# An expert block on one core: all six low halves of an expert's weights on VectorE, both halves of its output scaled by ScalarE

## The chip, the cores and the metric

The kernel runs on one core of one Trainium2 chip. The metric is the device time of one execution in microseconds (us), smaller is better. The engines are named as in the profile: PE is TensorE, PEld its weight loads, DVE is VectorE, ACT is ScalarE, POOL is GpSimd, SP is the engine that issues most DMAs.

## What is computed

One layer of an encoder block on 512 tokens of width 1024, all in float32: a norm, one wide projection, a gated delta rule (branch A), a sparse attention with an indexer (branch B), their gated sum through an output projection, and then a mixture of experts, which the change concerns:

```python
def hier_moe(h, w_rg, b_rg, w_re, b_re, w1, w3, w2):
    ...                                   # top-1 of 4 groups, then top-2 of its 4 experts
    act = jax.nn.silu(jnp.einsum("nd,edf->nef", xt, w1)) * jnp.einsum("nd,edf->nef", xt, w3)
    act = act * comb[:, :, None].astype(act.dtype)
    y = jnp.einsum("nef,efd->nd", act, w2)
    return y.reshape(bsz, s, d)
```

There are 16 experts, each with w1 and w3 of 1024 x 256 and w2 of 256 x 1024. A final norm follows.

## The kernel before

**Split products.** Every float32 matrix product is made of three products of a shorter format. `split` (line 151) makes a high half with an ACT copy (line 154) and a low half, source minus high half, with a subtraction on a chosen engine (line 155); `mm3` multiplies high x high, high x low and low x high. In the trace the weights' halves are `whi` and `wlo`, 128 x 1024 each. So every piece of the weights costs one ACT and one DVE or POOL instruction before PE can use it.

**The weights as a stream.** `plan` (from line 216) lists all pieces of weights in the order of use, each with its sources and with the engine that makes its low half. `feed_raw` issues the loads on SP, `feed` calls `halves` (line 293), which takes a pair of buffers and calls `split`. An expert has six pieces: four with 256 rows of w1 and w3 side by side, and two halves of w2. In `plan` the w2 pieces of an expert come behind the four pieces of the next one (lines 250 to 253). The engine of the low half is `(DVE, POOL, DVE)[i % 3]`, so pieces 1 and 4 of each expert go to POOL and the other four to DVE: 32 of the 96 pieces on POOL. The halves lie in a ring of six pairs of buffers, the raw pieces in a much longer one.

**One expert.** The loop from line 1686 goes over the 16 experts. Up to 128 tokens of an expert are gathered from DRAM by an indirect DMA on POOL (`gather`, line 1372), two experts ahead. `turn` transposes them on PE (line 1528) and `halves_x` writes their halves (`xhl`, ACT at line 1534, DVE at line 1535). `up` makes 24 products of 128 x 512. `glu` is the Silu on ACT (line 1547) and a product on DVE (line 1548); both write `a`. Then `finish` runs the expert before: `down` (line 1568) makes two outputs of 128 x 512, six products each, and scales them by the tokens' weights into `yb`: the left half on DVE (line 1573), the right half on ACT (line 1571). `scatter` (line 1576) adds `yb` into DRAM, again an indirect DMA on POOL. Last, `turn_a` transposes `a` on PE (line 1554) and splits it into `ah` (ACT) and `al_` (DVE). PE thus runs, for each expert: 24 products with eight transposes of the next expert's tokens among them, 12 products of the expert before, two transposes of `a`.

**The last two experts** are not scattered: `finish` keeps their scaled halves in SBUF (lines 157 and 158), and `combine` multiplies them with 0/1 matrices, which come from `sel` tiles (DVE, line 1368) transposed on PE (line 1706). In the sixth expert `more_tiles` (from line 1590) counts on DVE, in about 18 small instructions, whether an expert has more than 128 tokens; the code for such an overflow (`further`) is in loops at the end, whose instructions do not show up in the profiled execution.

**The order of instructions** on each engine is made by the tile framework when the program is built, so a change of an instruction's engine also moves others. Each engine then runs its own list in order.

Of the kernel before, what the change touches and what calls it, by code (L numbers as in the profile page):

```python
# [10 lines left out]
AF = mybir.ActivationFunctionType  # L11
OP = mybir.AluOpType
# [87 lines left out]
def body(tc, x, positions, norm1_g, w_in, w_proj_a, w_proj_b, w_out, norm2_g,  # L100
# [3 lines left out]
    PE, ACT, DVE, POOL, SP = nc.tensor, nc.scalar, nc.vector, nc.gpsimd, nc.sync  # L104
# [71 lines left out]
    def acc_tile():  # L176
        return pacc([128, 512], name="acc", tag="acc", bufs=4)
# [38 lines left out]
    plan, raws, ready, state = [], [], [], {"at": 0, "limit": None}  # L216
# [27 lines left out]
    def expert_pieces(w1, w3, w2):  # L244
        return [[w[sub * 256:(sub + 1) * 256, :] for w in (w1, w3)] for sub in range(4)] + [
            [w2[:, cb * 512:(cb + 1) * 512]] for cb in range(2)]

    W1, W3, W2 = w_exp_gate[0], w_exp_up[0], w_exp_down[0]

    order = [(e + d, i) for e in range(-1, 16) for d, i in ((1, 0), (1, 1), (1, 2), (1, 3), (0, 4), (0, 5)) if 0 <= e + d < 16]  # L250
    for e, i in order:
        o = ORDER[e]
        plan.append(("ex", expert_pieces(W1[o], W3[o], W2[o])[i], (DVE, POOL, DVE)[i % 3]))
    state["limit"], state["rawlimit"] = NIN + 4, NIN + 1
    LATE0 = NIN + 8 + 3 + NRAW
    late = [(stream, 3)] * 2
# [542 lines left out]
    def t8(name, pool=M):  # L799
        return pool([128, T, 8], name=name)  # L800

    beta, gg = t8("beta"), t8("gg")
    al, ex, u1, sp = (t8(n, AT_) for n in ("al", "ex", "u1", "sp"))
# [415 lines left out]
    def e1(shape, name, dt=F32):  # L1219
        return E1([128] + shape, dt, name=name)  # L1220
# [15 lines left out]
    for fb in range(4):  # L1236
        acc = acc_tile()
# [21 lines left out]
    nm, ex, sums, wn = e1([T, 2], "nm"), e1([T, 24], "exl"), e1([T, 3], "sums"), e1([T, 16], "wn")  # L1259
# [164 lines left out]
    for t in range(T):  # L1424
        acc = acc_tile()
# [134 lines left out]
    def product(al2, w):  # L1560
        ah, al_ = al2
        hi, lo, n = w
        acc = acc_tile()
        for k in range(2):
            mm3(acc, ah[:, k], al_[:, k], hi[:, k], lo[:, k], k == 0, k == 1)
        return acc

    def down(al2, y, cb, w, wtc):
        acc = product(al2, w)
        if cb:  # L1570
            ACT.activation(y[:, cb * 512:(cb + 1) * 512], acc, AF.Copy, scale=wtc)
        else:
            DVE.tensor_scalar(y[:, cb * 512:(cb + 1) * 512], acc, wtc, None, op0=OP.mult)

    def scatter(y, idc):
        return ins_of(POOL.indirect_dma_start(out=accd, out_offset=bass.IndirectOffsetOnAxis(ap=idc, axis=0), in_=y, in_offset=None,  # L1576
# [41 lines left out]
    def further(kv):  # L1618
        ek = SP.value_load(eki[0:1, bass.ds(kv, 1)], min_val=0, max_val=15)
        sl = ohk[:, bass.ds(kv, 1), :].to_broadcast([128, T, 16])  # L1620
        ofs = E2([128, 1], name="ofs", tag="ofs", bufs=1)
        DVE.tensor_copy(ofs, offk[:, bass.ds(kv, 1), :].rearrange("p a b -> p (a b)"))
        t16 = E2([128, T, 16], name="t16", tag="t16", bufs=1)
        pk_ = E2([128, T, 1], name="pk_", tag="pk_", bufs=1)
        rwf = E2([128, T, 2], name="rwf", tag="rwf", bufs=1)
        rwk = E2([128, T, 4], F32R, name="rwk", tag="rwk", bufs=1)
        for src, dst in ((posm, pk_), (f32(WT[:, :, :, 0]), rwf[:, :, 0:1]), (f32(WT[:, :, :, 1]), rwf[:, :, 1:2])):
            DVE.tensor_tensor(t16, src, sl, op=OP.mult)
            DVE.tensor_reduce(dst, t16, axis=AX.X, op=OP.add)
        DVE.tensor_copy(rwk[:, :, 0:2], C("tok")[:, :, None].to_broadcast([128, T, 2]))  # L1630
        DVE.tensor_copy(rwk[:, :, 2:4], rwf)
        DVE.tensor_scalar(pk_, pk_, ofs, None, op0=OP.subtract)
        idk = E2([128, 1], I32, name="idk", tag="idk", bufs=1)
        wtk = E2([128, 1], name="wtk", tag="wtk", bufs=1)
        look_up(slots_of(lambda t: pk_[:, t]), rwk, idk, wtk)
        gather(idk, xeb[0])
        for hf in range(2):
            turn(xeb[0], 0, hf)
        w = lambda W: W[bass.ds(ek, 1)].rearrange("e k c -> (e k) c")
        pieces = expert_pieces(w(W1), w(W3), w(W2))  # L1640
        acc = acc_tile()
        for sub in range(4):
            up(acc, 0, sub, halves(*load(pieces[sub]), DVE))
        al2 = turn_a(glu(acc))
        for cb in range(2):
            down(al2, yb[:, 0], cb, halves(*load(pieces[4 + cb]), DVE), wtk)
        scatter(yb[:, 0], idk)
# [11 lines left out]
    def finish(e):  # L1659
        if e < 16 - NP:  # L1660
            y = yb[:, e % 2]
            for cb in range(2):
                down(act[e], y, cb, chunk(e, 4 + cb), wts[:, ORDER[e]:ORDER[e] + 1])
            sent.append(scatter(y, ids[:, ORDER[e]:ORDER[e] + 1]))
            for i in range(max(0, e - 3), e):
                tc.declare_no_dep(sent[e], sent[i], reason="tokens of another group")
            return
        yhl[e] = yh, yl = spare_tile(F32R), spare_tile(F32R)
        for cb in range(2):
            split(yh[:, half[cb]], yl[:, half[cb]], product(act[e], chunk(e, 4 + cb)), scale=wts[:, ORDER[e]:ORDER[e] + 1])  # L1670
# [15 lines left out]
    for e in range(16):  # L1686
        acc = acc_tile()
# [107 lines left out]
```

## Time and profile before

| | |
|---|---|
| three runs | 748.82, 749.26 and 755.03 us; median 749.26 |
| the profiled execution | 749.99 us, span in the trace 747.9 us |
| mean granted TensorE clock | 0.966 |
| experts' stage (first product to last) | about 541 to 727 us |
| busy over the span | PE 669.9, DVE 553.6, ACT 408.2, POOL 352.5 us |

How to read it. The page cuts the span into 40 slices and groups instructions by line, engine and tile. A group's row ends with its busy time, the mean of one instruction in ns, then the time for which its engine stood idle just before it and what it was waiting for. A timeline row has the start, the duration, the engine, the line and the tile, and in brackets the idle time ahead of it and the instruction that ended it. A row of the stretches (windows) has the length and then for each engine its busy time and in brackets its number of instructions; then the granted clock, the DMA engines' busy share and GB/s. The average over the span says little here, because the stages have different limits; the stage of the experts has to be read by itself.

### The profile page before, as it was taken

The numbers are of one execution on the slowest core, as the hardware profiler recorded it, in microseconds if no ns is written. First come the engines' busy times: TensorE is split into PE (matmuls) and PEld (weight loads), VectorE is DVE, ScalarE is ACT, GpSimd is POOL, SyncE is SP. The second block draws the span as 40 slices with busy tenths as digits, with TensorE's granted clock in tenths as the row PEclk, the third lists the DMA queues.
The fourth block names the chain that finished last, engine by engine and source line by source line (L and its number), as shares of the span: only waits on it lengthen the run. The fifth ranks groups of instructions, "written<-read, shape, count | busy, mean of one in ns | idle before, by whom it ended". The sixth has DMA issues, their size and how long they took to land.

```text
span 747.9 us, 10556 instructions
## 1 busy us (share of the span) xinstructions
PE 669.9 (90%) x3460; PEld 544.0 (73%) x3460; DVE 553.6 (74%) x1112; ACT 408.2 (55%) x722; POOL 352.5 (47%) x300
## 2 busy tenths in 40 slices
PE   3999887889989999999799998999989997899792
PEld 3888666557757777778579998888967776687661
DVE  4562789999985556536954776656799998999785
ACT  5443365585979653443233423343558875888544
POOL 3217526456222212554451114731459985999343
PEclk9999988999999999999899999999999998999997
DMA  7333111112011223225144008697799999995233
GB/s 254 110 107 107 57 57 57 56 58 85 29 57 57 57 61 89 60 74 157 56 132 151 1 2 312 236 345 261 249 308 311 317 301 317 299 292 154 55 122 114
DMA packets 84025, 110.76 MB, mean 148 GB/s; under 512 B 17435, under 2 KB 57883, under 8 KB 83840
## 3 DMA queue, kind: packets, MB, share of 16 engines
q1 hardware_dynamic: 79360, 101.70, 42.2%
q0 software_dynamic: 4320, 7.77, 4.4%
q8 instruction: 28, 0.46, 0.3%
q10 hardware_dynamic: 288, 0.59, 0.2%
q14 instruction: 29, 0.24, 0.1%
HBM read 101.22 MB, written 16.78 MB: 158 GB/s over the span
## 4 chain that ended last, share of the span: by engine, by line
PE 45%; DVE 30%; DMA 11%; issue 7%; ACT 3%; POOL 2%; SPq 1%; DVEq 0%; ACTq 0%; POOLq 0%
PE acc L130 32%; PE pm L130 5%; DVE wlo L155 5%; DVE xh L447 4%; DVE ltmp L938 3%; DVE sn L595 3%; DVE m L594 3%; DVE sn L585 2%; ACT whi L154 2%; DMA g<-in_w_exp_up_dram 2%; DMA g<-in_w_exp_down_dram 2%; DVE X L939 1%; DMA spare<-in_w_exp_up_dram 1%; DMA x<-in_x_dram 1%; PE po L130 1%
## 5 line engine op out<-in xcount | busy, mean ns | idle before, releaser
L155 POOL TENSOR_TENSOR wlo<-raw,whi 128x1024 fp32r<-128x1024 f32 (+1 forms) x56 | 144.7, 2593 | 147.1 <-ACT whi L154 142.4
L154 ACT ACTIVATE whi<-raw 128x1024 fp32r<-128x1024 f32 (+1 forms) x123 | 127.4, 1049 | 111.3 <-PE acc L130 88.5
L155 DVE TENSOR_TENSOR wlo<-raw,whi 128x1024 fp32r<-128x1024 f32 (+1 forms) x67 | 115.6, 1738 | 38.9 <-ACT whi L154 37.4
L130 PE MATMUL acc<-hTh,wlo 128*128 128x512 f32 x224 | 90.9, 407 | 6.2 <-DVE wlo L155 5.8
L130 PE MATMUL acc<-hTh,whi 128*128 128x512 f32 x224 | 91.9, 410 | 5.1 <-ACT xh L445 4.2
L130 PE MATMUL acc<-whi,xhl 128*128 128x512 f32 x256 | 94.0, 420 | 0.3 <-DVE xhl L1535 0.3
L130 PE MATMUL acc<-hTl,whi 128*128 128x512 f32 x224 | 90.3, 403 | 0.0
L130 PEld LDWEIGHTS acc<-whi,xhl 128*128 128x128 f32 x256 | 49.8, 195 | 10.6 <-DVE xhl L1535 0.8
L130 PEld LDWEIGHTS acc<-hTh,whi 128*128 128x128 f32 x224 | 43.9, 196 | 18.1 <-ACT xh L445 5.0
L130 PEld LDWEIGHTS acc<-hTh,wlo 128*128 128x128 f32 x224 | 43.6, 195 | 17.1 <-DVE wlo L155 7.0
L130 PE MATMUL acc<-wlo,xhl 128*128 128x512 f32 x128 | 51.5, 402 | 0.0
L130 PEld LDWEIGHTS acc<-hTl,whi 128*128 128x128 f32 x224 | 43.5, 194 | 10.3 <-issue 1.7
L130 PE MATMUL acc<-whi,hTh 128*128 128x456 f32 (+1 forms) x120 | 46.2, 388 | 0.0
L130 PE MATMUL acc<-wlo,hTh 128*128 128x456 f32 (+1 forms) x120 | 44.9, 374 | 0.0
L130 PE MATMUL acc<-whi,hTl 128*128 128x456 f32 (+1 forms) x120 | 44.7, 373 | 0.0
L1576 POOL DMA_INDIRECT accd<-yb,ids x14 | 32.0, 2283 | 10.0 <-ACT ah L154 4.3
L1372 POOL DMA_INDIRECT xe<-h2d,ids x15 | 24.4, 1629 | 13.2 <-PE pm L1528 9.2
L447 DVE SCALAR_TENSOR_TENSOR xh<-xrb,sm,xh 128x511 f32<-128x511 f32 (+2 forms) x36 | 30.2, 895 | 0.0
L594 DVE MAX8 m<-sn 128x8 f32<-128x256 f32 (+2 forms) x48 | 26.7, 557 | 2.1 <-POOL sn L587 1.4
L130 PE MATMUL acc<-wlo,ah 128*128 128x512 f32 x64 | 26.5, 415 | 1.8 <-DVE wlo L155 1.8
L130 PEld LDWEIGHTS acc<-wlo,xhl 128*128 128x128 f32 x128 | 25.2, 197 | 3.9
L938 DVE TENSOR_TENSOR ltmp<-X,LN 128x31 f32<-128x31 f32 (+15 forms) x31 | 21.0, 676 | 8.7 <-DMA LN<-lane_n 7.8
(472 smaller groups left out, 1708.4 us busy)
## 6 DMA issues: line engine op xcount, KB each, us to landing
raw<-in_w_in_dram SPq DMA_DIRECT2D x24, 512.0 KB
raw<-in_w_exp_gate_dram SPq DMA_DIRECT2D x42, 256.0 KB
raw<-in_w_exp_up_dram SPq DMA_DIRECT2D x42, 256.0 KB
raw<-in_w_exp_down_dram SPq DMA_DIRECT2D x21, 512.0 KB
raw<-in_w_in_dram SPq DMA_DIRECT2D x16, 256.0 KB
raw<-in_w_out_dram SPq DMA_DIRECT2D x8, 512.0 KB
raw<-in_w_in_dram SPq DMA_DIRECT2D x8, 456.0 KB
x<-in_x_dram SPq DMA_DIRECT2D x4, 512.0 KB
```

The source lines that it names most:

```text
L130: return ins_of(PE.matmul(o, l, r, start=start, stop=stop, skip_group_check=True))
L154: h = ins_of(ACT.activation(hi, src, AF.Copy))
L155: return h, ins_of((lo_eng or DVE).tensor_tensor(lo, src, f32(hi), op=OP.subtract))
L447: DVE.scalar_tensor_tensor(xh[:, j:], xr[:, :512 - j], cw[:, blk, 3 - j:4 - j], xh[:, j:], op0=OP.mult, op1=OP.add)
L585: DVE.scalar_tensor_tensor(s, r[:, :N], iwn[:, h:h + 1], s, op0=OP.mult, op1=OP.add)
L594: DVE.max(m8, sn[t])
L595: DVE.match_replace(out=sn[t], in_to_replace=m8, in_values=sn[t], imm_value=-2 * BIG)
L938: DVE.tensor_tensor(tv, skew(flat[0], 0, n, d, 1), skew(flat[1], d, n, d, 32), op=OP.mult)
L939: DVE.tensor_reduce(skew(flat[0], d, n, 1, 1), tv, axis=AX.X, op=OP.add)
L1372: return ins_of(POOL.indirect_dma_start(out=xe, out_offset=None, in_=h2d[0:128 * tiles], in_offset=bass.IndirectOffsetOnAxis(ap=idc, axis= ...
L1576: return ins_of(POOL.indirect_dma_start(out=accd, out_offset=bass.IndirectOffsetOnAxis(ap=idc, axis=0), in_=y, in_offset=None, bounds_chec ...
```

## The change

Both edits are in the stage of the experts. The low halves of all six pieces of each expert are made by DVE. Both halves of `yb` are scaled by ACT.

```diff
@@ -250,7 +250,7 @@
     for e, i in order:
         o = ORDER[e]
-        plan.append(("ex", expert_pieces(W1[o], W3[o], W2[o])[i], (DVE, POOL, DVE)[i % 3]))
+        plan.append(("ex", expert_pieces(W1[o], W3[o], W2[o])[i], DVE))
@@ -1567,10 +1567,7 @@
     def down(al2, y, cb, w, wtc):
         acc = product(al2, w)
-        if cb:
-            ACT.activation(y[:, cb * 512:(cb + 1) * 512], acc, AF.Copy, scale=wtc)
-        else:
-            DVE.tensor_scalar(y[:, cb * 512:(cb + 1) * 512], acc, wtc, None, op0=OP.mult)
+        ACT.activation(y[:, cb * 512:(cb + 1) * 512], acc, AF.Copy, scale=wtc)
```

The lines below the second edit have numbers smaller by three in the changed kernel. The lists of the engines change as follows.

DVE, from the third expert's tokens to the `a` of the fourth (a row is line, operation, output<-inputs, shape; `wlo` is a low half of weights and the tile behind the arrow the place of the raw piece; `xhl` tokens, `al_` the low half of `a`). Before:

```order
L1548 TENSOR_TENSOR a<-a,acc 128x256
L1573 TENSOR_SCALAR yb<-acc,wts 128x512
L155 TENSOR_TENSOR wlo<-xr_4268,whi 128x1024
L155 TENSOR_TENSOR al__5469<-pm,ah 128x256
L155 TENSOR_TENSOR wlo<-spare_4882,whi 128x1024
L155 TENSOR_TENSOR wlo<-xr_4270,whi 128x1024
L1535 TENSOR_TENSOR xhl_5115<-pm,xhl_5115 128x512
L155 TENSOR_TENSOR wlo<-xr_4272,whi 128x1024
L1535 TENSOR_TENSOR xhl_5115<-pm,xhl_5115 128x512
L1548 TENSOR_TENSOR a<-a,acc 128x256
```

And changed:

```order
L1548 TENSOR_TENSOR a<-a,acc 128x256
L155 TENSOR_TENSOR wlo<-raw,whi 128x1024 x2
L155 TENSOR_TENSOR al__5469<-pm,ah 128x256
L155 TENSOR_TENSOR wlo<-xr_4268,whi 128x1024
L155 TENSOR_TENSOR wlo<-spare_4882,whi 128x1024 x2
L1535 TENSOR_TENSOR xhl_5115<-pm,xhl_5115 128x512
L155 TENSOR_TENSOR wlo<-xr_4270,whi 128x1024
L1535 TENSOR_TENSOR xhl_5115<-pm,xhl_5115 128x512
L1548 TENSOR_TENSOR a<-a,acc 128x256
```

From one `a` to the next the list holds six low halves instead of four and no `yb`; two low halves now stand ahead of `al_` instead of one and a `yb`, and `a` still follows the second `xhl` directly.

ACT, in the same place, from the Silu of an expert to the next one's tokens (`whi` is a high half of weights). Before:

```order
L1547 ACTIVATE a<-acc 128x256
L154 ACTIVATE whi<-xr_4268 128x1024
L154 ACTIVATE whi<-spare_4882 128x1024
L1571 ACTIVATE yb<-acc,wts 128x512
L154 ACTIVATE ah<-pm 128x256
```

And changed:

```order
L1547 ACTIVATE a<-acc 128x256
L154 ACTIVATE whi<-xr_4268 128x1024
L1570 ACTIVATE yb<-acc,wts 128x512
L154 ACTIVATE whi<-spare_4882 128x1024
L1570 ACTIVATE yb<-acc,wts 128x512
L154 ACTIVATE ah<-pm 128x256
```

The left half of `yb` comes in between the two high halves, so that one high half, the right `yb` and `ah` stand behind it.

POOL, from the gather of the fourth expert's tokens on (`accd<-yb` is the scatter). Before:

```order
L1372 DMA xe_4279<-h2d,ids 128x1024
L155 TENSOR_TENSOR wlo<-raw,whi 128x1024
L1372 DMA xe_4278<-h2d,ids 128x1024
L155 TENSOR_TENSOR wlo<-raw,whi 128x1024 x2
L1576 DMA accd<-yb,ids 512x1024
L155 TENSOR_TENSOR wlo<-raw,whi 128x1024
L1372 DMA xe_4279<-h2d,ids 128x1024
L155 TENSOR_TENSOR wlo<-spare_4882,whi 128x1024
L1576 DMA accd<-yb,ids 512x1024
```

And changed:

```order
L1372 DMA xe_4279<-h2d,ids 128x1024
L1372 DMA xe_4278<-h2d,ids 128x1024
L1573 DMA accd<-yb,ids 512x1024
L1372 DMA xe_4279<-h2d,ids 128x1024
L1573 DMA accd<-yb,ids 512x1024
```

POOL keeps the gathers and scatters and loses every subtraction between them. One more low half, that of the second piece of the first expert, moves to DVE ahead of the stage, in front of the line-1447 instruction, between the output projection's two column halves.

## The prediction

> **What bounds the kernel now.** I read the page first. Over the whole span PE is busiest, and the three costliest groups are the halves of weights:
>
> ```profile
> PE 669.9 (90%) x3460; PEld 544.0 (73%) x3460; DVE 553.6 (74%) x1112; ACT 408.2 (55%) x722; POOL 352.5 (47%) x300
> ```
>
> The change is in the experts' stage alone, so I cut that into stretches. Two neighbouring experts, from one transposition of `a` to the next, look like this:
>
> ```profile
> 574.90:586.10 11.20, 9.66 (x47) 7.58 (x45) 11.20 (x10) 9.03 (x12) 10.77 (x5) 1.00 0.96 300
> 586.10:595.60 9.50, 9.49 (x46) 7.77 (x47) 8.90 (x10) 7.89 (x10) 8.23 (x4) 1.00 1.02 326
> ```
>
> The columns are length, then busy time of PE, PEld, DVE, ACT and POOL, granted clock, DMA share, GB/s. In the shorter stretch PE is busy for 9.49 of 9.50 us: this is the pace that PE itself allows. In the longer one PE has the same work but DVE is busy for 11.20 of 11.20 us, so DVE sets the pace there. Next, who waited for whom from 541 to 728 us:
>
> ```profile
> PE pm L1554 <- DVE a L1548: 13.8, 8, 4.7
> PE pm L1706 <- DVE sel L1368: 4.0, 1, 4.0
> PE pm L1528 <- DMA xe<-h2d,ids: 2.3, 1, 2.3
> PE acc L130 <- DVE wlo L155: 1.8, 1, 1.8
> ```
>
> (total, times, longest). PE's waits for DVE add up to 13.8 + 4.0 + 1.8 = 19.6 us; the gather's 2.3 us is at the start of the stage. The timeline shows why DVE is late:
>
> ```profile
> 574.92 2.42 POOL L155 TENSOR_TENSOR wlo<-spare,whi 128x1024 fp32r<-128x1024 f32 x1 [0.28 <-ACT whi L154]
> 575.23 3.19 DVE L155 TENSOR_TENSOR wlo<-xr,whi 128x1024 fp32r<-128x1024 f32 x1
> 577.50 2.37 POOL L1576 DMA_INDIRECT accd<-yb,ids  x1 [0.17 <-DMA raw<-in_w_exp_gate_dram]
> 578.67 1.21 DVE L155 TENSOR_TENSOR wlo<-spare,whi 128x1024 fp32r<-128x1024 f32 x1
> 579.37 2.94 POOL L155 TENSOR_TENSOR wlo<-x2T,whi 128x1024 fp32r<-128x1024 f32 x1
> 579.81 3.59 DVE L155 TENSOR_TENSOR wlo<-xr,whi 128x1024 fp32r<-128x1024 f32 x1
> ```
>
> The same subtraction takes DVE 1.21 us beside a scatter, but 3.19 and 3.59 us beside a subtraction on POOL. It ends 1.1 us after POOL's does (578.42 against 577.34, 583.40 against 582.31), as if it had only then begun. So a low half on POOL costs DVE some 2 to 2.4 us, more than the 1.21 us for which DVE makes it itself.
>
> **The change part by part.** *Low halves.* DVE's largest group of low halves in this stage (busy, mean; then its least, median and longest), and the left halves of `yb`:
>
> ```profile
> L155 DVE TENSOR_TENSOR wlo<-raw,whi 128x1024 fp32r<-128x1024 f32 x41 | 80.6, 1978 | 3.7 <-ACT whi L154 2.2 <-DMA h<-in_w_exp_up_dram 0.6 <-DMA raw<-in_w_exp_gate_dram 0.6
> L155 DVE TENSOR_TENSOR wlo<-raw,whi x41: 1208/1224/5915, 542.7 to 720.0; 128x1024 fp32r<-128x1024 f32 x41
> L1573 DVE TENSOR_SCALAR yb<-acc,wts 128x512 f32<-128x512 f32 x14 | 10.3, 739 | 0.0
> ```
>
> The mean is 1978 ns, but minimum and median are 1208 and 1224: half are undisturbed, the rest carry the excess, up to 5915. POOL's subtractions all go, and no other POOL instruction that reads two tiles runs in this stage but the small `wr` at its start, so I price each of the six per expert at 1.21. Back to back they are closer still, as starts show:
>
> ```profile
> 583.92 1.21 DVE L155 TENSOR_TENSOR wlo<-xr,whi 128x1024 fp32r<-128x1024 f32 x1
> 585.05 0.68 DVE L1535 TENSOR_TENSOR xhl<-pm,xhl 128x512 fp32r<-128x512 f32 x1
> 585.65 0.41 DVE L1548 TENSOR_TENSOR a<-a,acc 128x256 f32<-128x256 f32 x1
> 585.98 0.74 DVE L1573 TENSOR_SCALAR yb<-acc,wts 128x512 f32<-128x512 f32 x1
> ```
>
> 1.13, 0.60 and 0.33 us from start to start. An expert then needs of DVE 6 x 1.13 + 2 x 0.60 + 0.33 for `a` and as much for `al_` = 8.6 us, without `yb`, against PE's 9.5: from DVE setting the pace it turns to 0.9 us to spare per expert. And `a` need not be there at once, since PE first runs the 12 products of the expert before:
>
> ```profile
> 581.60 0.40 PE L130 MATMUL acc<-whi,ah 128*128 128x512 f32 x1
> 584.16 0.40 PE L130 MATMUL acc<-whi,al__5469 128*128 128x512 f32 x1
> ```
>
> Eleven starts in 2.56 us, so 12 take 2.8. So PE's waits go, but not all. These rows carry what I leave:
>
> ```profile
> 556.88 0.44 PE L1554 MATMUL pm<-cst,a 128*128 128x128 f32 x2 [1.21 <-DVE a L1548]
> 609.75 0.17 DVE L1599 TENSOR_SCALAR lw<-miss 128x16 f32<-128x16 f32 x1
> 610.69 0.27 DVE L1605 TENSOR_TENSOR ohk<-cst,lw 128x112 f32<-128x112 f32 x1
> ```
>
> ```profile
> L1368 DVE TENSOR_TENSOR sel<-cst,posm 128x128 fp32r<-128x128 f32 x8 | 3.3, 441 | 0.2 <-PE pm L1706 0.2
> ```
>
> In the first expert two low halves now stand ahead of `a`, and I leave 0.5 of its 1.2 us; in the sixth and seventh some 18 counting instructions of 0.17 to 0.27 us (3 to 4 us) meet 1.8 us of spare, and I leave 1.7 of the longest wait, 4.7. The eight `sel` are 3.3 us more in the last experts: I leave 1.0 of 4.0, and 0.3 of the last 1.8. Gone: 11.6 + 3.0 + 1.5 = **16.1 us** (bounds: 8, if half stay, and 19.6).
>
> *The clock.* After the long waits PE is slow for a while:
>
> ```profile
> 621.20:626.00 4.80, 4.71 (x13) 3.80 (x14) 3.72 (x6) 2.39 (x3) 1.81 (x1) 0.52 0.92 320
> 697.40:701.00 3.60, 3.53 (x11) 2.76 (x12) 2.42 (x6) 1.28 (x3) 0.00 (x0) 0.53 0.00 0
> 721.50:725.00 3.50, 3.47 (x11) 2.71 (x11) 1.78 (x4) 1.07 (x2) 0.00 (x0) 0.52 0.95 375
> ```
>
> At a granted clock of 0.52, 4.8 us hold 2.5 us of full-speed work, so they cost 2.3; the others 1.7 each, 5.7 together. The first two follow the waits of 4.7 and 4.0 us, which shrink to 1 or 2; I take those two, **4.0 us**, and leave the third, in the tail, as it is (bounds 0 and 5.7). The Trainium skill, "TensorE: Matmul & The Clock Gate", Part 1, says that the gate falls to half after an idle window of about 3.4 us and reopens after as long a busy one. By that rule only the first two waits cost anything, and the sum is the same; but the trace also shows 0.52 behind the 1.8 us wait near 720, so by the rows even a short rest may cost.
>
> *The scaling.* ACT gets 14 left halves of `yb` at the price of the right ones, and these are what else it does and waits for:
>
> ```profile
> L1571 ACT ACTIVATE yb<-acc,wts 128x512 f32<-128x512 f32 x14 | 9.6, 689 | 4.6 <-PE acc L130 4.6
> L154 ACT ACTIVATE whi<-raw 128x1024 fp32r<-128x1024 f32 x57 | 59.5, 1061 | 11.1 <-PE acc L130 8.1 <-issue 1.8 <-PE pm L130 0.3
> ```
>
> In the two stretches above ACT is busy for 9.03 + 7.89 = 16.9 us for two experts; with two more `yb` it is 18.3 of PE's 19.0. That fits, barely, and the list is in order: the left `yb` waits for the first six products, and behind it stand a high half, the right `yb`, `ah` and three more high halves, for which DVE's low halves wait. The cover is the ring, which lets ACT run ahead:
>
> ```profile
> 576.92 1.06 ACT L154 ACTIVATE whi<-xr 128x1024 fp32r<-128x1024 f32 x1
> 586.30 0.48 PE L130 MATMUL acc<-whi,xhl 128*128 128x512 f32 x1
> ```
>
> By the order of the pieces that high half is the first of the fifth expert; PE uses it 9.4 us later. A few tenths of delay in ACT stay in there. Without this cover each left `yb` would cost its 0.69 us, 9.6 in all. Bounds 0 and 9.6; I take **2.0**, nearer to 0, since ACT's own idle is mostly waiting for PE to release buffers (8.1 us above).
>
> *Moved or freed elsewhere, at nothing.* POOL's gathers and scatters no longer queue behind subtractions, so they come earlier:
>
> ```profile
> DMA to landing us min/median/max: 5.1/7.3/7.9
> ```
>
> A gather lands at most 7.9 us after its issue, and is now issued as soon as its tile is free, which is more than one expert (9.5 us) ahead of use. The one low half that moves ahead of the stage was POOL's at 500.32 and now meets a DVE that stands idle there:
>
> ```profile
> 500.32 2.39 POOL L155 TENSOR_TENSOR wlo<-raw,whi 128x1024 fp32r<-128x1024 f32 x1 [10.79 <-ACT whi L154]
> 505.13 0.69 DVE L1267 SCALAR_TENSOR_TENSOR xr<-acc,xr 128x512 f32<-128x512 f32 x1 [4.15 <-PE acc L130]
> ```
>
> If that cover were gone it would cost 1.2 us. SP's loads could bound a faster stage, so I looked at their end:
>
> ```profile
> 671.28 2.00 SPq L289 DMA_DIRECT2D raw<-in_w_exp_down_dram  x2
> 710.64 0.48 PE L130 MATMUL acc<-whi,xhl 128*128 128x512 f32 x1
> ```
>
> ```profile
> 680.00:684.00 4.00, 4.00 (x21) 3.29 (x20) 3.40 (x4) 3.38 (x6) 3.85 (x2) 1.00 0.33 87
> ```
>
> The last weights have landed by about 682, when the DMA share drops to 0.33, and the last expert's products start at 710.6. They would have to start 25 us earlier before the loads held them up. The tail's reload of the sums follows the last scatter, which moves forward with the stage.
>
> **The sum.** -16.1 - 4.0 + 2.0 = -18.1 us. Against the profiled execution (749.99) that gives 731.9; the median of the runs is 0.7 lower, so I predict **731 us**, 2.4% less. That is over the 1% that a measurement of this kernel can tell from no change.
>
> **The rivals.**
>
> *ACT becomes the bound.* For it: 18.3 of 19.0 us, in order, behind PE five times per expert. Against it: nine microseconds of lead for the high halves. If all of ACT's idle in the shorter stretch (9.5 - 7.9 = 1.6 us) is waiting that stays, an expert takes 7.9 + 0.7 + 1.6 = 10.2 us, 0.7 above PE's pace; over 14 experts that is 9.8 us where I took 2.0: 731 + 8 = **739 us**. If half of it stays (9.4 us) nothing is lost.
>
> *DVE stays late.* If only half of the 19.6 us of waits goes and the clock stays (because the counting and `sel` instructions, or a late `whi`, hold `a` up), the gain is 9.8 us: **740 us**. For it: only 0.9 us of spare per expert. Against: the stretches without a wait ran with DVE at 8.9 of 9.5 us and PE never stopped.
>
> *Slower: DVE's long subtractions are not POOL's doing*, but come from the DMAs' writes or ACT's, and all 94 in the stage take the present mean. By the plan 31 of these come from POOL and 63 are DVE's already (one of each runs ahead of the stage), so DVE's load changes by 31 x 1.98 - 10.3 = +51 us. In every second expert DVE has 0.6 us to spare, some 5 us; the rest lengthens the stage: 749 + 46 = **about 795 us**. It decides from the mean at which 94 equal the present 63 x 1.98 + 10.3 = 135 us, that is 1.44 us. Against it: 1.21 us was reached with the DMAs at 300 GB/s, and each long one shown ends 1.1 us after POOL's.
>
> That the change does not do what it says is excluded by the lists of the engines.
>
> **How the numbers follow.** Forecast 0.70 (its own range 726 to 738), ACT as the bound 0.14, DVE still late 0.11, slower 0.05. The lower end takes all 19.6 and 5.7 us and no cost, 749.99 - 25.3 = 724.7, rounded to 725; the upper end takes in both mild rivals, 741. Faster by over 1% (below 741.8): nearly all of the forecast and most of the two mild rivals, 0.89; within 1%: what is left of these, 0.06; slower 0.05.
>
> **What would show each step right or wrong.** Right: no line-155 row on POOL behind 500 us, DVE's `wlo` at 1.21 us with a maximum below 1.5, experts 9.5 to 9.8 us apart, the waits of PE for `a` below 3 us, no granted clock near 0.5 in the middle of the stage, two `yb` groups' worth (28) on ACT. ACT would be guilty if PE's or DVE's waits for ACT rows grew and ACT were busy throughout; DVE, if it were still busy in all of a stretch; the third rival, if `wlo` rows stayed above 1.4 us with POOL free. The prediction is wrong if the time is above 741 or if the gain comes from elsewhere than PE's waits.

## The result and the profile after

The changed kernel takes 724.75 us (median of 4 runs, 722.27 to 726.03) against 750.45 for the kernel before (median of 4, 748.82 to 755.03): a ratio of 0.964, 95% interval 0.962 to 0.967. That is 25.7 us less. The forecast was 731, and the time lies 0.25 us below the lower end of its range, 725. The profiled execution of the changed kernel took 722.27 us with a span of 720.1, the shortest of its four. (Ratios, here and below, leave disturbed executions out, so they need not be the quotient of the medians.)

The first line of the page after:

```profile
PE 660.6 (92%) x3460; PEld 539.8 (75%) x3460; DVE 531.5 (74%) x1130; ACT 412.9 (57%) x736; POOL 258.9 (36%) x268
```

PE's share rises from 90% to 92% with the same 3460 instructions. POOL is freed of 94 us, and DVE, which took over 32 subtractions, is busy for *less* time than before (531.5 against 553.6 us).

The same cut by stretches as in the prediction (length, busy time of PE, PEld, DVE, ACT, POOL, granted clock, DMA share, GB/s): two ordinary experts, the one with the counting instructions, and the last one.

```profile
579.60:589.00 9.40, 9.40 (x47) 7.70 (x46) 8.90 (x11) 8.74 (x13) 3.78 (x2) 1.00 0.98 316
627.80:637.30 9.50, 9.50 (x48) 7.76 (x47) 9.00 (x11) 8.84 (x13) 3.77 (x2) 1.00 0.96 281
...
589.00:599.40 10.40, 10.40 (x55) 8.62 (x54) 10.40 (x15) 8.85 (x13) 2.85 (x2) 1.00 0.89 272
685.60:694.20 8.60, 8.60 (x40) 6.95 (x39) 8.06 (x10) 6.97 (x10) 1.55 (x1) 1.00 0.47 146
```

There are no longer two kinds of expert. PE is busy in all of every stretch; DVE needs 8.9 to 9.0 us, ACT 8.7 to 8.8. In the expert with the counting DVE is busy throughout too, but PE has 0.9 us more work of its own there and does not wait. What PE waited for, from the stage's start to just behind its last transposition of `a`:

```profile
PE pm L1528 <- DMA xe<-h2d,ids: 0.9, 1, 0.9
PE acc L130 <- ACT ah L154: 0.3, 1, 0.3
PE acc L130 <- DVE xhl L1535: 0.3, 1, 0.3
```

All of the 19.6 us for `a`, `sel` and `wlo` are gone. The wait for the gather, 2.3 us before, is 0.9. The timeline of DVE in an ordinary expert, and the low halves of the whole stage (least, median and longest duration in ns, then first and last start):

```profile
582.71 1.22 DVE L155 TENSOR_TENSOR wlo<-h,whi 128x1024 fp32r<-128x1024 f32 x1
584.42 0.69 DVE L1535 TENSOR_TENSOR xhl<-pm,xhl 128x512 fp32r<-128x512 f32 x1 [0.50 <-ACT xhl L1534]
585.03 1.22 DVE L155 TENSOR_TENSOR wlo<-xr,whi 128x1024 fp32r<-128x1024 f32 x1
586.25 0.69 DVE L1535 TENSOR_TENSOR xhl<-pm,xhl 128x512 fp32r<-128x512 f32 x1
```

```profile
L155 DVE TENSOR_TENSOR wlo<-raw,whi x61: 1204/1216/1291, 544.1 to 692.6; 128x1024 fp32r<-128x1024 f32 x61
L155 DVE TENSOR_TENSOR wlo<-xr,whi x12: 1209/1216/1226, 571.8 to 672.0; 128x1024 fp32r<-128x1024 f32 x12
```

The longest is 1.29 us, where it was 5.9. ACT's two groups that matter:

```profile
L154 ACT ACTIVATE whi<-raw 128x1024 fp32r<-128x1024 f32 x57 | 59.0, 1060 | 5.5 <-PE acc L130 2.7 <-ACT xhl L1534 2.0 <-PE pm L130 0.3
...
L1570 ACT ACTIVATE yb<-acc,wts 128x512 f32<-128x512 f32 x28 | 19.2, 687 | 1.9 <-PE acc L130 1.2
```

Twenty-eight halves of `yb` at 0.69 us, as priced, and ACT's idle time ahead of the high halves fell from 11.1 to 5.5 us: the added work went into it.

### The profile page after: what moved, and what is told of

The parts are those of the page before. It is cut to its first block, busy times and chain, and to the rows that moved or that the text cites. A ratio compares the mean times of both kernels' runs of the same rounds, so it can differ in the third digit from the quotient of the medians.

```text
span 720.1 us, 10544 instructions
## 1 busy us (share of the span) xinstructions
PE 660.6 (92%) x3460; PEld 539.8 (75%) x3460; DVE 531.5 (74%) x1130; ACT 412.9 (57%) x736; POOL 258.9 (36%) x268
## 4 chain that ended last, share of the span: by engine, by line
PE 61%; DVE 22%; POOL 5%; issue 4%; DMA 4%; ACT 3%; SPq 0%; POOLq 0%; DVEq 0%; ACTq 0%
PE acc L130 47%; PE pm L130 5%; DVE xh L447 4%; DVE sn L595 3%; DVE ltmp L938 3%; DVE m L594 3%; DVE sn L585 2%; PE pm L1528 2%; POOL wlo L155 1%; DVE X L939 1%; POOL mTl L1209 1%; DMA x<-in_x_dram 1%; PE po L130 1%; ACT whi L154 1%; DMA xe<-h2d,ids 1%
## 5 line engine op out<-in xcount | busy, mean ns | idle before, releaser
L155 DVE TENSOR_TENSOR wlo<-raw,whi 128x1024 fp32r<-128x1024 f32 (+1 forms) x88 | 110.5, 1282 | 36.3 <-ACT whi L154 29.5
L155 POOL TENSOR_TENSOR wlo<-raw,whi 128x1024 fp32r<-128x1024 f32 (+1 forms) x35 | 89.0, 2542 | 124.0 <-ACT whi L154 107.0
L130 PE MATMUL acc<-whi,xhl 128*128 128x512 f32 x256 | 91.3, 410 | 0.3 <-DVE xhl L1535 0.3
L130 PEld LDWEIGHTS acc<-whi,xhl 128*128 128x128 f32 x256 | 48.1, 188 | 10.1 <-DVE xhl L1535 0.8
L1573 POOL DMA_INDIRECT accd<-yb,ids x14 | 23.9, 1704 | 58.7 <-ACT ah L154 58.7
L1372 POOL DMA_INDIRECT xe<-h2d,ids x15 | 22.5, 1498 | 42.4 <-PE pm L1528 35.7
L130 PE MATMUL acc<-whi,mTh 128*128 128x512 f32 (+1 forms) x72 | 27.4, 380 | 1.1 <-DVE ma L1203 1.1
```

The source lines that it names most:

```text
L130: return ins_of(PE.matmul(o, l, r, start=start, stop=stop, skip_group_check=True))
L155: return h, ins_of((lo_eng or DVE).tensor_tensor(lo, src, f32(hi), op=OP.subtract))
L1372: return ins_of(POOL.indirect_dma_start(out=xe, out_offset=None, in_=h2d[0:128 * tiles], in_offset=bass.IndirectOffsetOnAxis(ap=idc, axis= ...
```

## Experiments: which of the two edits

**The first edit alone** (low halves on DVE, left `yb` still on DVE):

```
-        plan.append(("ex", ...[i], (DVE, POOL, DVE)[i % 3]))
+        plan.append(("ex", ...[i], DVE))
```

> All six low halves on VectorE, the left halves of yb still on VectorE too (the first of the two edits alone). Theory A, the two-input subtraction on GpSimd blocks the one on VectorE and its removal is the whole gain: VectorE is busy for 132.2 of 139.3 us in the changed kernel's stage, and 14 left halves add 0.33 (from start to start) to 0.74 us (by duration) each, 136.8 to 142.6 us, so the time is 725 to 729 us and no wait of PE for `a` exceeds 1 us. Theory B, VectorE becomes the bound without the second edit: 730 to 736 us, with waits of PE for `a` back in most experts. All subtractions of low halves in the stage at 1.2 us by A and B alike.

Measured 728.82 us (ratio 0.971, 0.967 to 0.975). Theory A, at its upper end; no wait of PE for `a` at all is left. The low halves are worth some 22 of the 25.7 us.

**The second edit alone** (both halves of `yb` on ACT, two low halves on POOL):

> Both halves of yb scaled by ScalarE, two of six low halves still on GpSimd (the second of the two edits alone). Theory A: the subtractions on VectorE are still as long as 3 to 6 us beside those on GpSimd; the slow experts (11.2 us apart) lose 0.33 to 0.74 us each, seven or eight of them, so the time is 744 to 749 us. Theory B, the scaling was what VectorE lacked: below 735 us.

Measured 749.32 us (ratio 0.998, 0.9955 to 1.0005): 0.3 us above theory A's range, and not to be told from no change. The two large waits are nearly what they were:

```profile
PE pm L1554 <- DVE a L1548: 11.9, 9, 4.6
PE pm L1703 <- DVE sel L1368: 4.1, 1, 4.1
```

So the second edit earns nothing that shows by itself, but 4.1 us (728.82 to 724.75) behind the first, a difference at which the intervals of the two ratios (0.967 to 0.975 and 0.962 to 0.967) only just touch. Below, the traces show where it is earned.

**Half of the first edit** (one of six low halves on POOL, both `yb` on ACT):

```
+        plan.append(("ex", ...[i], POOL if i == 4 else DVE))
```

> The changed kernel with one of six low halves per expert (the fifth piece) on GpSimd again, where the kernel before had two. Theory A, each subtraction on GpSimd that meets one on VectorE costs VectorE about 2 us and saves it 1.13: 9.0 + 0.9 = 9.9 us per expert against PE's 9.47, less than half of the way back to the kernel before: 727 to 734 us, with low halves on VectorE of 3 us again, one per expert. Theory B, one per expert still fits because VectorE had 0.5 us to spare or the collision can be missed: 723 to 726 us.

Measured 731.32 us (ratio 0.974, 0.970 to 0.978), inside theory A's range. PE waits for `a` again:

```profile
PE pm L1554 <- DVE a L1548: 6.2, 5, 3.1
```

One low half per expert on POOL costs 6.6 us, two cost 24.6 (749.32), which is more than in proportion. With one, 13 low halves on DVE take more than 1.35 us and together lose 13.5 us; with two, 27 of them lose 47.6. Theory A's working, the same loss in every expert, did not hold: from the eighth expert to the twelfth DVE's subtraction meets only the end of POOL's (1.75 us instead of 1.21), DVE is busy for 8.3 of 9.5 us and PE loses nothing. The time is lost in the first experts, around the counting and in the last ones.

## Experiments: what on POOL blocks DVE

These five take the changed kernel and give POOL work that nothing uses, on a dead tile (the ring of raw weights has one tile less for it). First two subtractions per expert:

```
+            if sub in (1, 3) and e < 14:
+                POOL.tensor_tensor(dm, dm, dm, op=OP.subtract)
```

> The changed kernel, and per expert (the first 14) two subtractions 128x1024 on GpSimd of a tile from itself, which nothing else uses; the ring of raw weights has one tile less to make room. Theory A, the block between the two engines needs nothing but that GpSimd reads tiles from SBUF at the time: each costs VectorE about 2.2 us, 9.0 + 4.4 = 13.4 us per expert against PE's 9.47, 55 us over 14 experts if none of it is hidden: 760 to 785 us, with subtractions on VectorE of 3 us and more. Theory B, the long subtractions came from something else (the shared tile `whi`, the loads, the order of the pieces): 724 to 729 us and all low halves at 1.2 us.

Measured 764.82 us (ratio 1.020, 1.016 to 1.024): theory A. (The 28 subtractions did not stay two to an expert: POOL had run them all by 631 us, in the first six experts.) With one input in its place:

```
+                POOL.tensor_scalar(dm, dm, 1.0, None, op0=OP.mult)
```

> As the run with two subtractions per expert on GpSimd, but each is a multiplication by 1.0 with one input, 128x1024. Theory A1, any instruction of GpSimd that reads SBUF blocks the two-input subtraction on VectorE for its length: 740 to 785 us by how long it takes, with low halves above 2 us. Theory A2, only two inputs on both sides collide: 724 to 729 us, low halves at 1.2 us.

Measured 768.85 us, inside A1, but this run does not show it: PE waited 33 us for gathers and only 1.6 us for `a`. The instructions had been laid three or four together between a gather and a scatter, and POOL's queue became the bound. So both were made again with the two instructions tied behind the expert's gather, and a third with an instruction that only writes.

```
-                gather(...)
+                sg = gather(...)
+                with after_(sg):
+                    for _ in range(2):
+                        POOL.tensor_tensor(dm, dm, dm, op=OP.subtract)   # or tensor_scalar, or memset
```

> As the run with two subtractions per expert on GpSimd, but the two now stand right behind the expert's gather (13 experts, 26 subtractions), so that gathers and scatters don't queue behind three or four of them. Theory A, the block needs nothing but GpSimd reading SBUF: the unpaced run cost 40 us for 28, 1.4 us each; so 26 cost 30 to 45 us, 755 to 770 us, and each low half that meets one ends 1.1 us after it. Theory B, the unpaced run was slow because GpSimd's own queue was full: 725 to 735 us.

> The same with a multiplication by 1.0, one input, in place of each subtraction. In the unpaced run PE waited 33 us for gathers, so its time tells nothing of VectorE, but low halves that met one ended 0.66 us before it did, so they seemed blocked for its first part only, about 0.9 us of 2.8. Theory A1, one input blocks too, for that shorter time: 26 x 0.9 less what VectorE has to spare, 735 to 748 us, waits of PE for gathers below 3 us. Theory A2, one input does not block: 724 to 729 us.

> The same with a memset of 128x1024 on GpSimd, which reads nothing. If reading is what blocks VectorE: 723 to 728 us, as the changed kernel, and all low halves below 1.35 us. If any GpSimd instruction blocks: above 735 us. It also shows whether the ring of raw weights with one tile less costs anything.

| POOL's 26 instructions | us | ratio to before (95%) |
|---|---|---|
| subtraction, two inputs | 761.44 | 1.011 (1.005 to 1.017) |
| multiplication, one input | 743.18 | 0.989 (0.985 to 0.993) |
| memset, none read | 724.11 | 0.964 (0.960 to 0.967) |
| none (the changed kernel) | 724.75 | 0.964 (0.962 to 0.967) |

Theory A, A1 and the first expectation of the third hold. One collision of each kind, in the timelines (start, duration; `x2` are two back to back). Two inputs:

```profile
585.91 4.75 POOL L1694 TENSOR_TENSOR h<-h 128x1024 f32<-128x1024 f32 x2
...
589.76 1.98 DVE L155 TENSOR_TENSOR wlo<-x2T,whi 128x1024 fp32r<-128x1024 f32 x1
591.66 1.21 DVE L155 TENSOR_TENSOR wlo<-xr,whi 128x1024 fp32r<-128x1024 f32 x1
```

One input:

```profile
582.30 5.67 POOL L1694 TENSOR_SCALAR h<-h 128x1024 f32<-128x1024 f32 x2
...
585.29 2.01 DVE L155 TENSOR_TENSOR wlo<-x2T,whi 128x1024 fp32r<-128x1024 f32 x1
587.23 1.21 DVE L155 TENSOR_TENSOR wlo<-xr,whi 128x1024 fp32r<-128x1024 f32 x1
```

Only written:

```profile
578.54 1.99 POOL L1694 MEMSET h<- 128x1024 f32 x2
...
578.47 1.22 DVE L155 TENSOR_TENSOR wlo<-x2T,whi 128x1024 fp32r<-128x1024 f32 x1
579.61 1.22 DVE L155 TENSOR_TENSOR wlo<-xr,whi 128x1024 fp32r<-128x1024 f32 x1
```

Beside two inputs DVE ends 1.08 us after POOL (591.74 against 590.66), as in the kernel before: it has waited to POOL's end. Beside one input it ends 0.67 us *before* POOL does (587.30 against 587.97), so it was held only for POOL's first part. Beside the memset it is not held at all. These distances are the same each time: all 27 low halves over 1.35 us in the kernel before, and all 25 in the run with two inputs, end 1.08 or 1.09 us after one of POOL's subtractions, and all 23 in the run with one input end 0.65 to 0.67 us before POOL's multiplication. The group of low halves from `raw` tells the same over each whole stage, in the columns count, busy time, mean in ns, idle time ahead. With two inputs on POOL:

```profile
L155 DVE TENSOR_TENSOR wlo<-raw,whi 128x1024 fp32r<-128x1024 f32 x51 | 85.6, 1707 | 0.0
```

With one:

```profile
L155 DVE TENSOR_TENSOR wlo<-raw,whi 128x1024 fp32r<-128x1024 f32 x57 | 80.1, 1431 | 1.2 <-ACT whi L154 1.2
```

With the memset:

```profile
L155 DVE TENSOR_TENSOR wlo<-raw,whi 128x1024 fp32r<-128x1024 f32 x64 | 75.9, 1218 | 2.8 <-ACT whi L154 1.9 <-issue 0.8
```

The mean falls from 1707 to 1431 to 1218 ns, the undisturbed duration.

The dead tile is no tile that DVE reads, so the shared `whi` is not needed to make the subtractions long; nor are the loads enough, since the changed kernel has the same ones and no low half above 1.29 us. The memset is shorter than the others (0.96 us against 2.3 and 2.8), so it tests fewer us of POOL, but those that it covers cost nothing. The Trainium skill, "SBUF — State Buffer", section "Who interferes with whom", says that a DVE instruction with two SBUF inputs contends with a GpSimd instruction that reads SBUF and not with one that only writes it; these three runs agree. Its section "SBUF: two separate sides" also says that of two such instructions the one that starts first has the port for the whole of it and the other is blocked; the whole instruction fits the two inputs here, not the one. Nor does the order of the starts settle it in these traces. In the kernel before, DVE's subtraction at 578.67, in the prediction's timeline, started 0.70 us ahead of POOL's and was not held (1.21 us, and POOL's took 2.94). This one started 0.52 us ahead and was:

```profile
560.38 4.03 DVE L155 TENSOR_TENSOR wlo<-raw,whi 128x1024 fp32r<-128x1024 f32 x1
560.90 2.42 POOL L155 TENSOR_TENSOR wlo<-raw,whi 128x1024 fp32r<-128x1024 f32 x1
```

## Experiments: ACT, the counting, and the stages ahead

**ACT's room.** Two copies more per expert on ACT, beyond the change:

```
         ACT.activation(y[:, ...], acc, AF.Copy, scale=wtc)
+        ACT.activation(dm[:, ...], dm[:, ...], AF.Copy)
```

> The changed kernel, and ScalarE copies a 128x512 tile onto itself behind each half of yb (28 copies more, two per expert, used by nothing; the ring one tile less). ScalarE is busy for 126.1 of 139.3 us in the stage, 0.9 us to spare per expert, and two copies of 0.69 are 1.38. Theory A, ScalarE can use its spare time and the ring covers the rest of its lateness: 14 x 0.5 = 7 us at most, 725 to 733 us. Theory B, as the prediction feared, its list is in order and behind PE, so that each copy costs in full: 19 us, 740 to 746 us.

Measured 722.43 us (ratio 0.961, 0.957 to 0.965): below theory A's range; no cost shows. The stretches of two ordinary experts:

```profile
581.70:591.20 9.50, 9.50 (x48) 7.75 (x47) 9.21 (x11) 9.50 (x15) 3.86 (x2) 1.00 1.00 320
629.90:639.40 9.50, 9.50 (x48) 7.75 (x47) 9.50 (x12) 9.50 (x15) 3.03 (x2) 1.00 0.89 272
```

ACT is busy for 9.50 of 9.50 us and PE still is too. That ACT's list stands in order behind PE cost nothing even with no idle time left: what the prediction argued from the ring's lead it should have believed, and it put 2.0 us on it all the same.

**Where the second edit earns its 4 us.** In the kernel with the first edit alone an ordinary expert, the one with the counting, and the next but one look like this:

```profile
571.70:581.20 9.50, 9.50 (x48) 7.77 (x47) 8.92 (x12) 8.34 (x11) 3.52 (x2) 1.00 1.00 308
600.20:612.00 11.80, 10.56 (x47) 7.60 (x46) 11.80 (x29) 8.35 (x11) 2.61 (x2) 1.00 1.02 311
621.80:632.80 11.00, 10.94 (x52) 8.61 (x51) 10.95 (x14) 9.14 (x12) 4.23 (x2) 1.00 0.93 292
```

The ordinary expert has PE's pace, 9.5, with DVE at 8.92. With the counting DVE is busy for 11.80 of 11.80 us and sets the pace there, as in the kernel before; two experts later it is busy nearly throughout once more (10.95 of 11.00). Two kernels leave the counting out, with its results set to zero (which they are for these inputs). The first:

```
-            more_tiles()
+            for v in (ohk, offk, eki):
+                DVE.memset(v, 0)
```

> The low halves all on VectorE and the left halves of yb on VectorE too (728.8 us in its own run), and the counting instructions in the sixth expert left out (they count the tokens beyond 128 per expert; their results are set to zero, which they are for these inputs). Theory A, the second edit is worth its 4 us only where VectorE has extra work, at the counting and at the `sel`: without the counting 723.5 to 726.5 us, of which 0.9 us is PE's own counting products. Theory B, the left halves of yb cost a little in every expert: 727 to 728.5 us.

Measured 732.29 us, neither theory. It lost its time ahead of the stage: the first product of the experts starts at 550.95 us where the same kernel with the counting has 543.19. The whole list of instructions is laid anew when a few are taken out, and there PE now waits 2.68 us for a low half at 494 us and has two stretches of slow clock, at 494.8 and 542.6 us, that the other does not have. Inside the stage it was faster, so it was tried once more, without and with the second edit, the zeros now tied to the stage.

> The counting left out again (its three results set to zero inside the stage this time), low halves all on VectorE, left halves of yb on VectorE. In the earlier run without the counting the stage itself was 152.7 us long from its first product to the last transposition of `a`, against 158.0 with the counting and 151.6 in the changed kernel, but the program came 8 us late to the stage. Theory A, the second edit earns its time at the counting alone: the stage 152 to 153 us again, and the whole within 1.5 us of the same kernel with both edits. Theory B, it earns it in every expert: 3 us and more behind that kernel.

> The changed kernel with the counting left out in the same way. The sixth expert takes 0.9 us longer than the others in the changed kernel though PE never waits there: those are the counting's own products. So the stage 150.5 to 151 us, the whole 0 to 2 us below the changed kernel, unless the program comes later to the stage as in the earlier run without the counting; the difference to the kernel with one edit counts here.

Measured 731.51 and 726.79 us, 4.7 apart, so by the whole times theory B; the second kernel's own forecast was missed too (2.0 us above the changed kernel, not 0 to 2 below). But both came late to the stage again (546.78 and 545.72), 1.1 us apart, and PE waited for the first gather in both, 2.29 us with a slow clock behind it in the first, 1.99 us without one in the second. The steady part of the stage, from the first to the last transposition of `a`, is free of that:

| | counting | no counting |
|---|---|---|
| first edit alone | 144.6 | 141.1 and 141.8 |
| both edits | 139.3 | 139.6 |

The second edit is worth 5.4 us there with the counting (144.64 against 139.27): 3.4 in the fifth to eighth expert, around the counting, and 1.9 in the last three, which have the `sel`. It is worth 1.5 to 2.2 without: 0.7 in the last three experts and 0.8 or 1.5 in the fifth to eighth, for a reason that I did not trace. (139.6 holds a wait of 0.8 us for `sel` that the changed kernel does not have.) The other experts from the second to the twelfth take 9.44 to 9.50 us in all of them. So in the stage A holds for most of it: freeing DVE of `yb` pays where DVE has something extra to do. The whole times don't show it, and why leaving the counting out makes the program 3 to 8 us late ahead of the stage stays open beyond the waits and slow stretches named.

**The stages ahead.** All other low halves on DVE as well, 35 of them:

```
-LOWS = "PPDDPDPDDPDPPPDPPPPPPPPPPPPPPPPP"
+LOWS = "DDDDDDDDDDDDDDDDDDDDDDDDDDDDDDDD"
...
-    want("wo", w_out[0], 8, [(cb * 512, 512)], DVE, POOL, DVE)
+    want("wo", w_out[0], 8, [(cb * 512, 512)], DVE)
```

> The changed kernel, and all other low halves (35 ahead of the experts' stage) on VectorE too. Theory A, what holds in the experts' stage holds everywhere: each of the 35 on GpSimd costs VectorE more than 1.13 us, so the time falls to 712 to 722 us. Theory B, ahead of the stage most of them meet no two-input instruction of VectorE: in the trace of the changed kernel 13 of VectorE's instructions there are 1 to 2 us longer than the shortest of their kind beside one, some 20 us in all, and VectorE would have to take on 35 x 1.13 = 40 us; where it sets the end the time grows, 726 to 745 us.

Measured 722.46 us (ratio 0.962, 0.959 to 0.965): between the two theories, 2.3 us under the changed kernel with intervals that overlap. The page's first line:

```profile
PE 667.2 (93%) x3460; PEld 545.1 (76%) x3460; DVE 537.0 (74%) x1165; ACT 413.7 (57%) x736; POOL 181.4 (25%) x233
```

DVE took over 35 x 1.2 = 42 us of subtractions and is busy for only 5.5 us more (531.5 to 537.0). What it loses to POOL's subtractions ahead of the stage is thus nearly what they would cost it, about 37 us. My count of 20 us came from single rows that were much longer than the shortest of their kind; I left out the rows that the timeline gives together. Over all of DVE's instructions ahead of the stage that overlap one of POOL's in the changed kernel's trace, what they take beyond the shortest of their kind adds up to 32.5 us. The time shows no difference that could be measured.

> The changed kernel, and only those six low halves ahead of the experts' stage moved to VectorE beside which one of its instructions was 1.5 to 2 us longer (those that start on GpSimd at 148, 198, 204, 343, 348 and 373 us). Theory A, the block is the whole price there: 6 x (1.6 - 1.13) = 3 us saved, 720 to 724 us. Theory B, the list of instructions is laid anew around the moved ones and other pairs collide, or VectorE's own 1.13 us comes at a worse place: 724 to 730 us.

Six of them alone (`LOWS`, `LOWS_A` and `z` changed at those pieces): 723.32 us (ratio 0.964, 0.960 to 0.967), in A's range and in the changed kernel's. No version here beats the changed kernel by more than the measurement can tell.

## Why the prediction was right in kind and too small in size

| term, us | predicted | from the two traces |
|---|---|---|
| PE's waits for DVE | -16.1 | -19.5 |
| clock in the stage | -4.0 | -5.7 |
| scaling on ACT | +2.0 | 0 |
| products around the waits | 0 | -2.3 |
| ahead of the stage | 0 | +1.4 |
| the gather's wait | 0 | -1.4 |
| behind the last transposition | 0 | -0.3 |
| span | -18.1 | -27.8 |

The right column: the first product of the experts starts at 541.20 before and 542.62 after; from there to the last transposition of `a` it is 180.40 and 151.56 us; behind it 26.28 and 25.95. The products around the waits are what is left of the stage's 28.8 us when the other terms are taken off. The two traced executions are 27.8 us apart where the medians are 25.7 apart: the one of the changed kernel is the shortest of its four. Which terms are larger in it than in the others isn't shown.

**The bound and the low halves: right.** POOL's subtraction holds DVE's, and each of DVE's six falls to 1.21 us (measured 1.20 to 1.29). The third rival, 795 us, is excluded: with POOL free no row is above 1.29, under its 1.44. Ordinary experts are 9.47 us apart, just under "9.5 to 9.8".

**What failed: both sides of the second edit.** "I take 2.0, nearer to 0" was a mis-sized term of the sum: for the scaling on ACT no cost shows, and ACT took two copies more per expert at nothing (722.43). The same edit has another side that the sum gave no term: it takes 10.3 us from DVE. I had used that in the 8.6 us per expert, "without `yb`", and then still left 3.5 us of waits at the counting, the `sel` and the first expert. All of these went. With the first edit alone the stage from the first to the last transposition of `a` is 5.4 us longer than with both, around the counting and in the last three experts (some 1.5 us of it recorded as waits), and the whole measures 4.1 us more.

**The waits: the term mis-sized most, by 3.4 us** (16.1 for 19.5), for that reason. The two mild rivals fall: DVE is not late (no wait for `a`), ACT is not the bound (8.7 to 8.8 of 9.5 us, and no wait of PE for it above 0.3).

**The clock: mis-sized by 1.7 us.** I took two slow stretches and missed a third in the stage, 547.3 to 550.8, behind the gather's wait of 2.3 us; all three are gone, and the wait ahead of the missed one is 0.9 us now.

**What had no term.** The 2.3 us around the waits are products that run slower than their pace without being counted as waiting: experts of the kernel before without a wait take 9.52 to 9.54 us instead of 9.47, and those with one, where the clock was full, take 0.15 to 0.21 more than the wait and the pace. What the weight loads waited for in the stage before shows the same:

```profile
PEld pm L1554 <- DVE a L1548: 17.7, 9, 5.2
PEld pm L1706 <- DVE sel L1368: 4.7, 2, 4.4
PEld acc L130 <- DVE wlo L155: 2.2, 1, 2.2
```

24.6 us, where PE's own waits for these add up to 19.6. The range's lower end, "all 19.6 and 5.7 us and no cost", came to 724.7 and was rounded up to 725. It held every term that I had, but not this one: with it the end is 722.4.

**Ahead of the stage** the low half that moved to DVE, at 499.51, costs nothing, as said: at 532 us the changed kernel is 0.2 us ahead. Then comes a stretch of slow clock that the profile before does not have there:

```profile
530.33:533.74 3.41, 2.52 (x25) 1.00 0.98 312
533.74:537.16 3.42, 3.42 (x18) 0.50 0.81 270
537.16:540.57 3.41, 3.41 (x32) 1.00 0.90 258
```

3.42 us at half speed are 1.7 us, and the stage starts 1.4 us late. Why the clock fell there stays open: PE had waited for only 0.9 us just before. The gather gives that back. Its first use by PE, before:

```profile
547.51 1.08 PE L1528 MATMUL pm<-cst,xe 128*128 128x128 f32 x4 [2.25 <-DMA xe<-h2d,ids]
```

And after:

```profile
547.48 0.63 PE L1528 MATMUL pm<-cst,xe 128*128 128x128 f32 x4 [0.89 <-DMA xe<-h2d,ids]
```

PE can go on at the same time in both, so coming 1.4 us later it waits 1.4 us less. That is chance, since the gather is issued 0.5 us later in the changed kernel (541.03 against 540.53), and the shorter wait is no gain of the change. **Behind the last transposition** the third slow stretch that I had left in the tail is gone as well. DVE's last instruction comes 0.9 us sooner behind that transposition (its end 19.16 us after it before, 18.24 after), but what follows it, the last transfers out among it, takes 0.6 us longer (7.1 and 7.7), so that the tail is only 0.3 us shorter.

## What to carry to other kernels

An elementwise instruction given to GpSimd that reads tiles is not free for VectorE: look in the timeline whether VectorE's two-input instructions beside it end just after it does, and charge VectorE for the hold, which here was more than doing the work itself. A relief of the engine that sets the pace has to be priced where that engine has extra work, not in the ordinary turn of the loop. A range's lower end should hold more than the sum of PE's recorded waits, since its weight loads wait longer and the products around a wait run slower.

## What the runs showed of the hardware that was not expected

**The clock changes at fixed instants, 3.413 us apart.** In every trace all changes of the granted clock lie on one grid of that step, within 0.03 us (in the kernel before from 458.6 to 724.8: 78 steps), but the grid starts elsewhere in each. The stage of the kernel before, cut along it (length, busy time of PE, granted clock, DMA share, GB/s):

```profile
615.61:619.02 3.41, 0.93 (x4) 1.00 1.03 303
619.02:622.44 3.42, 1.15 (x4) 0.50 0.95 331
622.44:625.85 3.41, 3.41 (x9) 0.50 0.97 338
625.85:629.26 3.41, 3.41 (x20) 1.00 1.07 340
...
673.64:677.05 3.41, 1.82 (x10) 1.00 0.93 329
677.05:680.47 3.42, 3.42 (x20) 1.00 0.72 252
```

A window with PE idle for 2.5 us is followed by one at half speed, and so is one at half speed with PE idle for 2.3 us; a window with 1.6 us idle is not. I counted PE's recorded waits in all windows of the experts' stage, from its first product to its last transposition of `a`, in all 16 traces. Of the windows at full speed, the 724 with up to 1.65 us of waits were all followed by full speed, the 20 with 1.98 us or more all by half speed, and of the ten between (1.72 to 1.92) six by half speed. Of the windows at half speed, all 13 with 1.1 us of waits or more were followed by another one, and 25 of the 27 with up to 0.72 by full speed. So in this stage a wait of PE costs its own length, and up to 1.7 us more when it fills somewhat over half of a window: the same wait of 2.0 us near 457 us fell into one window in the kernel before and cost a slow stretch, and across two in the changed kernel (from 454.47 to 456.50, with the edge at 455.24) and cost none.

That fits the half speed that the prediction saw behind a wait of 1.76 us near 720, one of the ten, and the waits of 1.5 to 1.6 us in the stage that left the clock alone. It does not explain the changed kernel's slow stretch ahead of the stage: the window in front of it, at 530.33, holds only 0.89 us of waits. It also holds products of only 24 columns, where the stage's main ones have 512; whether that counts is not shown. The Trainium skill, "TensorE: Matmul & The Clock Gate", Part 1, has a free-running window of 3413 ns, and the traces agree with the step; that somewhat over half a window of waits is enough is what the traces add.

**One input on POOL is slower than two.** The multiplication of 128x1024 by a constant takes 2.81 us on average in its run, the subtraction of two inputs 2.31, the memset 0.96:

```profile
L1694 POOL TENSOR_SCALAR h<-h 128x1024 f32<-128x1024 f32 x26 | 73.2, 2814 | 1.5
```

The subtraction:

```profile
L1694 POOL TENSOR_TENSOR h<-h 128x1024 f32<-128x1024 f32 x26 | 59.9, 2305 | 1.4
```

The memset:

```profile
L1694 POOL MEMSET h<- 128x1024 f32 x26 | 25.1, 964 | 0.8
```

The 2.31 is the mean of 14 subtractions at 1.89 to 1.96 us and 12 at 2.75 to 2.77; the multiplications take 2.77 to 3.02. Yet a multiplication holds DVE for less.
